# One decoder layer in fp32 on one core: the second MLP product's weights are loaded from POOL's queue

## The chip, the core and the metric

The kernel runs on one core of a Trainium2 chip. The metric is the device time of one execution in microseconds (us). TensorE (PE) multiplies, VectorE (DVE), ScalarE (ACT) and GpSimd (POOL) work on tiles, and SyncE (SP) does nothing but issue transfers (DMAs). POOL and ACT can issue DMAs as well. All DMAs of the core run on the same 16 DMA engines. The profile shows the DMAs that SP issues in queue q1 (hardware_dynamic) and those that POOL issues in queue q0 (software_dynamic).

## The reference

One layer, sequence 1024, width 1024, everything float32:

```python
h = x @ w_in                                  # columns: pool | q | k | v | forget gate
mix = concat(pool_mixer(h), forgetting_attention(h)) @ w_out
x = layer_norm(ALPHA * x + mix, ln1_g, ln1_b)
hid = square(relu(x @ w_mlp1))                # 1024 x 4096
x = layer_norm(ALPHA * x + hid @ w_mlp2, ln2_g, ln2_b)
```

The last line holds the second MLP product, `hid @ w_mlp2`: 1024 tokens by 4096 by 1024. Its weights are 16 MB, called `w2` in the kernel (`in_w_dram` in the profile, where the numbers in names are left out, so that `w1` and `w2` share that name).

## The kernel before

Every fp32 operand of a product is split into a high and a low part (`split`, L70: ACT makes the high part at L71, DVE the low one at L72), and each product is done as three matmuls. Both MLP products use a two-by-two block scheme with seven products in place of eight: the blocks of weights and activations are first added and subtracted into the versions B11, B21, T1 to T4 and B22 and A11 to A22, S1 to S4.

**First MLP product (`Unit`, L735, PE's line L727).** Sixteen units of 256 hidden columns. Each unit makes seven products, squares the result, forms the sums and splits them. POOL stores the split activations to `hid_dram` (L852 and L865, seven stores of 512 KB a unit). One unit, the kept one, stays in SBUF.

**Second MLP product (`Pair` and `Step`, L958 and L1020, PE's line L1060).** A `Pair` is the two 128-row blocks of `w2` that belong to a unit: `load_f` and `load_g` fetch 512 KB each into buffers of tag `S`, of which there are three (`NBUF`, L48). `split_b`, `sums`, `split_t2`, `split_t13` and `split_t4b` turn them into the seven weight versions. A `Step` is one group of two token tiles with up to four pairs, plus the kept unit in the first four steps. `Step.load` (L1028) brings the split activations back from `hid_dram` into buffers of tags `Q` and `A`, 256 KB a load, 128 KB for the group A22. `load_x` (L1047) brings a row tile of the first norm's output into an `S` buffer, to be added as the residual. Each step makes seven products (`p1` to `p7`), adds them to the rows `y`, and the last four steps norm and store them; there POOL multiplies and adds the norm's rows (`on_pool`, L601).

The steps of a pair are hung on places in the chain of units and steps: `load_f` and `load_g` on the step before the one that first uses the pair. For the pair that a step starts with, the code reads:

```python
at(i - 1, 4 * k, p.load_f)
at(i - 1, 2 + 3 * k, p.load_g)
at(i - 1, 3 + 3 * k, p.split_b)
```

Two things set the order. Each engine carries out its own instructions in the order in which a scheduler laid them down, and a DMA issue is an instruction of the engine that issues it: it waits in that engine's queue for its buffer to be free, and all that stands behind it in the queue waits with it. A load into an `S` buffer waits for the last split that reads the buffer's former contents.

Of the kernel before, what the change touches and what calls it, by code (L numbers as in the profile page):

```python
# [36 lines left out]
def trunk(ctx, tc, xT, xn, wuqk, wvf, bf, poolw, pscale, wout, g1, b1, w1, w2, g2, b2, out):  # L37
# [5 lines left out]
    nc = tc.nc  # L43
# [7 lines left out]
    def slot(tag, shape, dt=F32R):  # L51
        uid[0] += 1
        return sb.tile([P] + list(shape), dt, tag=tag, bufs=NBUF[tag], name=f"{tag}{uid[0]}")
# [9 lines left out]
    def bank(tag=None):  # L63
        uid[0] += 1
        if tag is None:
            tag = CYCLE[rr[0] % 8]
            rr[0] += 1
        return ps.tile([P, CH], F32, tag=tag, bufs=PBUF[tag], name=f"{tag}{uid[0]}")
# [134 lines left out]
    for t in range(4, NT):  # L203
        for half in range(2):
            b = bank()[:, 0:VW]
# [432 lines left out]
    for n, unit in enumerate(order):  # L638
        p = n // 8
# [95 lines left out]
    class Unit:  # L735
# [6 lines left out]
        def load_f(self):  # L742
            self.f = slot("S", [2, H, P], F32)
            nc.sync.dma_start(self.f.rearrange("p b k f -> p (b k) f"), w1[2 * self.u])

        def load_g(self, tag="S"):
            self.g = slot(tag, [2, H, P], F32)
            nc.sync.dma_start(self.g.rearrange("p b k f -> p (b k) f"), w1[2 * self.u + 1])
# [209 lines left out]
    class Pair:  # L958
# [4 lines left out]

        def load_f(self):
            self.f = slot("S", [2, CH], F32)
            nc.sync.dma_start(self.f.rearrange("p b n -> p (b n)"), w2[2 * self.u])

        def load_g(self, tag="S"):
            self.g = slot(tag, [2, CH], F32)
            nc.sync.dma_start(self.g.rearrange("p b n -> p (b n)"), w2[2 * self.u + 1])  # L970

        def put(self, name, hi, lo, raw):
            self.v[name] = (hi, lo)
# [285 lines left out]
```

## Time and profile before

| | us |
|---|---|
| median of 3 runs (1038.8 to 1041.12) | 1039.55 |
| profiled execution | 1042.56 |
| its span, first to last instruction | 1040.8 |
| PE busy in the span | 1019.3 |
| DVE busy | 757.1 |
| ACT busy | 514.1 |
| POOL busy | 154.7 |

The prediction's rows come from these views. A *timeline* row is: start in us, length in us, engine, line, operation, output<-inputs, shape, count, and in brackets the idle time of the engine before it with what ended it. "SPq" is SP's queue: its rows are issues. A *waits* row is: engine, line and tile that waited, what it waited for, us in total, number of times, longest. The *chain of waits* follows the work that ended last back in time: start, length, what. A *windows* row is a stretch, its length, then for PE, PEld (weight loads of PE), DVE, ACT and POOL the busy us with the number of instructions, then the granted clock of PE, the busy share of the 16 DMA engines and GB/s. A *groups* row has, after the bar, busy us and mean ns, and then the idle time before with its causes. A *DMA* row of a queue has packets, MB and share of the engines; one of an issue has count, KB each and median us from issue to landing.

### The profile page before, as it was taken

What the parts mean: (1) busy time and instruction counts of PE and PEld (TensorE: products, weight loads), DVE (VectorE), ACT (ScalarE), POOL (GpSimd) and SP (SyncE); (2) the same over time, 40 slices, a digit from 0 to 9 for tenths busy, and PEclk for the clock granted to TensorE, in tenths of its full rate; (3) what the DMA queues carried; (4) which work ended last, traced back from release to release, by engine and by line L of the source; (5) the groups of instructions that cost most, each with busy time, mean ns of one, the idle gap of its engine ahead of it and who ended that gap; (6) DMA issues with size and microseconds to landing.
All of it is one profiled execution on the core that took longest, in us unless ns stands there. A gap on an engine that the chain in (4) does not pass through costs nothing.

```text
span 1040.8 us, 14125 instructions
## 1 busy us (share of the span) xinstructions
PE 1019.3 (98%) x4976; PEld 847.3 (81%) x4976; DVE 757.1 (73%) x1300; ACT 514.1 (49%) x823; POOL 154.7 (15%) x267
## 2 busy tenths in 40 slices
PE   9999999999999999999999999999999999999996
PEld 9988888888768888887888888888788888888884
DVE  4776678677767887989778778888775666565547
ACT  4623666666664332676766766668521221122152
POOL 0200112111100031112122121120100000000047
PEclk9999999999999999999999999999999999999998
DMA  9702311112585523239667667665989888878753
GB/s 352 279 28 85 113 59 36 40 40 58 176 273 150 183 113 102 75 131 362 241 260 265 224 261 262 223 252 197 350 285 307 285 259 286 275 224 272 238 187 121
DMA packets 113670, 206.29 MB, mean 198 GB/s; under 512 B 9592, under 2 KB 78008, under 8 KB 113600
## 3 DMA queue, kind: packets, MB, share of 16 engines
q1 hardware_dynamic: 94608, 137.63, 41.1%
q0 software_dynamic: 18560, 67.12, 16.6%
q8 instruction: 39, 0.64, 0.3%
q10 hardware_dynamic: 432, 0.66, 0.2%
q14 instruction: 31, 0.25, 0.1%
HBM read 132.42 MB, written 72.94 MB: 197 GB/s over the span
## 4 chain that ended last, share of the span: by engine, by line
PE 50%; issue 4%; DVE 3%; DMA 1%; POOL 1%; SPq 0%; ACT 0%; DVEq 0%; POOLq 0%
PE s L1060 15%; PE pv L1060 8%; PE s L727 8%; PE mm L727 6%; PE pt L727 6%; PE pv L727 4%; PE pt L1060 2%; PE mm L1060 2%; DMA hid_dram<-A 1%; DMA A<-hid_dram 1%; DVE B L72 1%; POOL hid_dram L852 0%; POOL A L720 0%; SPq L1039 0%; DVE A L850 0%
## 5 line engine op out<-in xcount | busy, mean ns | idle before, releaser
L71 ACT CAST B<-S 128x1024 fp32r<-128x1024 f32 (+1 forms) x78 | 67.8, 881 | 163.2 <-PE s L1060 62.8
L727 PE MATMUL s<-B,Q 128*128 128x512 f32 x492 | 116.4, 389 | 0.2 <-ACT B L71 0.2
L727 PEld LDWEIGHTS s<-B,Q 128*128 128x128 f32 x492 | 92.3, 188 | 19.7 <-ACT B L71 0.7
L72 DVE TENSOR_TENSOR B<-S,B 128x1024 fp32r<-128x1024 f32 (+1 forms) x78 | 78.0, 1008 | 31.0 <-ACT B L71 30.8
L1060 PE MATMUL s<-B,Q 128*128 128x512 f32 x390 | 94.7, 389 | 0.0
L1060 PE MATMUL s<-B,A 128*128 128x512 f32 x333 | 84.0, 397 | 2.3 <-DMA A<-hid_dram 2.3
L1060 PEld LDWEIGHTS s<-B,Q 128*128 128x128 f32 x390 | 73.2, 188 | 15.5
L71 ACT CAST Q<-S 128x1024 fp32r<-128x1024 f32 x53 | 55.7, 1051 | 57.3 <-PE s L727 17.0
L852 POOL DMA_DIRECT2D hid_dram<-A x90 | 48.1, 537 | 221.4 <-ACT A L849 164.5
L1060 PEld LDWEIGHTS s<-B,A 128*128 128x128 f32 x333 | 63.1, 190 | 17.1 <-DMA A<-hid_dram 2.7
L72 DVE TENSOR_TENSOR Q<-S,Q 128x1024 fp32r<-128x1024 f32 x53 | 65.6, 1238 | 15.2 <-ACT Q L71 14.7
L727 PE MATMUL pt<-B,Q 128*128 128x512 f32 x312 | 74.6, 389 | 0.0
L727 PE MATMUL mm<-B,Q 128*128 128x512 f32 x300 | 71.6, 389 | 0.0
L727 PEld LDWEIGHTS pt<-B,Q 128*128 128x128 f32 x312 | 58.5, 188 | 12.1
L727 PEld LDWEIGHTS mm<-B,Q 128*128 128x128 f32 x300 | 56.3, 188 | 11.7
L377 ACT ACTIVATE A<-A,nm 128x1024 f32<-128x1024 f32 (+7 forms) x64 | 49.7, 777 | 32.3 <-DVE nm L375 31.0
L416 PE MATMUL pv<-A,B 128*128 128x256 f32 x320 | 62.2, 295 | 2.8 <-DVE A L399 1.2
L416 PEld LDWEIGHTS pv<-A,B 128*128 128x128 f32 x320 | 51.0, 188 | 17.1 <-ACT A L398 7.0
L399 DVE TENSOR_TENSOR A<-pt,A 128x512 fp32r<-128x512 f32 (+1 forms) x80 | 49.6, 634 | 15.1 <-ACT A L398 14.5
L850 DVE TENSOR_TENSOR A<-A,A 128x1024 f32<-128x1024 f32 x45 | 53.6, 1220 | 0.0
L362 POOL TENSOR_TENSOR A<-A,maskb 128x128 f32<-128x128 f32 x48 | 23.4, 491 | 190.8 <-DVE nm L375 135.2
L398 ACT CAST A<-pt 128x512 fp32r<-128x512 f32 (+1 forms) x80 | 41.5, 543 | 19.2 <-PE pt L397 18.3
(427 smaller groups left out, 2342.0 us busy)
## 6 DMA issues: line engine op xcount, KB each, us to landing
hid_dram<-A POOLq DMA_DIRECT2D x105, 512.0 KB, 4.0
S<-in_w_dram SPq DMA_DIRECT2D x62, 512.0 KB
Q<-hid_dram SPq DMA_DIRECT2D x101, 256.0 KB
A<-hid_dram SPq DMA_DIRECT2D x79, 256.0 KB
S<-in_wuqk_dram SPq DMA_DIRECT2D x12, 512.0 KB
wo_dram<-Q POOLq DMA_DIRECT2D x10, 512.0 KB, 3.8
B<-wo_dram SPq DMA_DIRECT2D x10, 512.0 KB
A<-ncf_dram SPq DMA_DIRECT2D x8, 512.0 KB
```

The lines of the kernel that those rows point to most:

```text
L71: nc.scalar.copy(hi, src)
L72: nc.vector.tensor_tensor(lo, src, hi.bitcast(F32), ALU.subtract)
L362: nc.gpsimd.tensor_tensor(nb[:, qs], nb[:, qs], maskb, ALU.add)
L377: nc.scalar.activation(pt[:, :nk], pt[:, :nk], AF.Exp, bias=nm, scale=-1.0, accum_out=rsum[h][:, i : i + 1])
L398: nc.scalar.copy(tt[:, 0, ev], tp[:, ev])
L399: nc.vector.tensor_tensor(tt[:, 1, ev], tp[:, ev], tt[:, 0, ev].bitcast(F32), ALU.subtract)
L416: nc.tensor.matmul(ov, V[j][:, h].rearrange("p s d -> p (s d)"), tt[:, s, a:b], start=(j == 0 and s == 0), stop=(j == 2 * m + 1 and s == 1),)
L727: nc.tensor.matmul(dst, b[x][:, k], A[a][y][:, k], start=first and k == 0 and i == 0, stop=k == H - 1 and i == 2, skip_group_check=not first,)
L850: nc.vector.tensor_tensor(x, x, hi.bitcast(F32), ALU.subtract)
L852: nc.gpsimd.dma_start(hid_dram[self.u, :, i, AT[name] : AT[name] + 2 * CH], part.rearrange("p q n t -> p (q n t)"))
L1060: nc.tensor.matmul(dst, h[:, p_], w[q_], start=first and u == self.us[0] and j == 0, stop=u == self.us[-1] and j == 2, skip_group_check=no ...
```

## The change

`Pair.load_f` and `Pair.load_g` issue their DMA from POOL's queue instead of SP's. Nothing else in the source is touched: sizes, buffers and what is computed stay.

```diff
         def load_f(self):
             self.f = slot("S", [2, CH], F32)
-            nc.sync.dma_start(self.f.rearrange("p b n -> p (b n)"), w2[2 * self.u])
+            nc.gpsimd.dma_start(self.f.rearrange("p b n -> p (b n)"), w2[2 * self.u])
 
         def load_g(self, tag="S"):
             self.g = slot(tag, [2, CH], F32)
-            nc.sync.dma_start(self.g.rearrange("p b n -> p (b n)"), w2[2 * self.u + 1])
+            nc.gpsimd.dma_start(self.g.rearrange("p b n -> p (b n)"), w2[2 * self.u + 1])
```

There are 32 such loads, one for each 128-row block of `w2`. The first of them that stand behind the last stores of the first product, on POOL (numbers in names are those of the buffers, `w2` stands under its own name here):

```order
 L852 DMA hid_dram_3781<-A1239_6906 128x1024
 L852 DMA hid_dram_3781<-A1232_6870 128x1024
+L966 DMA S1265_7030<-in_w2_dram 128x1024
+L970 DMA S1269_7056<-in_w2_dram 128x1024
+L966 DMA S1281_7133<-in_w2_dram 128x1024
+L970 DMA S1285_7163<-in_w2_dram 128x1024
```

After the last two stores POOL's queue now holds 26 weight loads in a row, up to the norms of the last steps. The six loads before these stand in pairs and fours between the stores of the last units.

The same place in SP's queue, where the first steps' activations are loaded:

```order
 L1039 DMA Q1262_7016<-hid_dram_3781 128x2x256 x2
-L966 DMA S1265_7030<-in_w2_dram 128x1024
 L1039 DMA Q1277_7115<-hid_dram_3781 128x2x256
 L1039 DMA A1264_7027<-hid_dram_3781 128x2x256 x2
 L1039 DMA A1268_7053<-hid_dram_3781 128x2x128 x2
-L1039 DMA A1272_7073<-hid_dram_3781 128x2x256
-L970 DMA S1269_7056<-in_w2_dram 128x1024
-L1039 DMA A1272_7073<-hid_dram_3781 128x2x256
+L1039 DMA A1272_7073<-hid_dram_3781 128x2x256 x2
 L1039 DMA A1273_7076<-hid_dram_3781 128x2x256
```

Two weight loads leave; the second stood between the two loads into the buffer A1272. The order of the activation loads themselves is the same here.

The scheduler also lays down a few of VectorE's instructions in another order, the first of them here (L1070 adds a product to the rows `y`, L72 splits, L985 begins a pair's sums):

```order
 L72 TENSOR_TENSOR B1267_7050<-S1249_6952,B1267_7050 128x1024
+L1070 TENSOR_TENSOR A1244_6931<-A1244_6931,pv1263_7019 128x512
 L72 TENSOR_TENSOR B1271_7068<-S1265_7030,B1271_7068 128x512
-L1070 TENSOR_TENSOR A1244_6931<-A1244_6931,pv1263_7019 128x512
+L72 TENSOR_TENSOR B1275_7109<-S1253_6971,B1275_7109 128x1024
 L985 TENSOR_TENSOR S1265_7030<-S1265_7030 128x512
-L72 TENSOR_TENSOR B1275_7109<-S1253_6971,B1275_7109 128x1024
 L986 TENSOR_TENSOR U1274_7085<-S1269_7056,S1265_7030 128x512
```

An addition and a split move ahead of work on the newly loaded buffer S1265. The split of S1253 (B1275_7109) is the last reader of the buffer into which the next weight load, S1281_7133, goes. PE's order is the same before and after.

## The prediction

> **What bounds the kernel now.** I read the engines' totals first, then the windows by stage, then PE's waits, and last the queues around the one wait that was left.
>
> ```profile
> PE 1019.3 (98%) x4976; PEld 847.3 (81%) x4976; DVE 757.1 (73%) x1300; ACT 514.1 (49%) x823; POOL 154.7 (15%) x267
> PE s L1060 <- DMA A<-hid_dram: 2.3, 1, 2.3
> ```
>
> The second row is all that PE waits for between 477 and 1027 us, in the two MLP products. The changed loads serve the second one, L1060, from 711 us on. So the change can win or lose there only by that one hole of 2.30 us, by what follows from it, or by opening new ones.
>
> ```profile
> 746.55 0.85 PE L1060 MATMUL s<-B,A 128*128 128x512 f32 x3
> 749.71 2.01 PE L1060 MATMUL s<-B,A 128*128 128x512 f32 x6 [2.30 <-DMA A<-hid_dram]
> 742.89 6.78 DMA A<-hid_dram
> 749.71 5.44 PE s L1060 x15
> 801.80 5.45 PE s L1060 x24
> 746.00:751.00 5.00, 2.70 (x12) 1.72 (x11) 1.98 (x4) 1.87 (x3) 0.00 (x0) 1.00 1.06 357
> 751.00:754.50 3.50, 3.50 (x10) 2.69 (x9) 2.85 (x4) 0.40 (x1) 0.00 (x0) 0.51 0.96 306
> ```
>
> The first two rows are PE's timeline, the next three the chain of waits, the last two windows (PE, PEld, DVE, ACT, POOL busy, granted clock, DMA share, GB/s). PE waits for an activation load that SyncE issued at 742.89 and that took 6.78 us to land. After the hole the granted clock is 0.51 for 3.5 us: 15 matmuls take 5.44 us, where 24 take 5.45 at the full clock (0.227 each, 3.41 for 15). So the hole costs 2.30 + (5.44 - 3.41) = **4.33 us** in this execution. A shorter hole costs no clock:
>
> ```profile
> 30.73 0.39 PE L83 MATMUL s<-A,B 128*128 128x260 f32 x1 [1.49 <-ACT B L71]
> 31.00:37.00 6.00, 6.00 (x51) 6.00 (x51) 6.00 (x15) 6.00 (x10) 1.03 (x2) 1.00 0.41 162
> ```
>
> 1.49 us of waiting left the clock at 1.00. The step is somewhere between 1.49 and 2.30 us.
>
> This execution took 1042.56 us (span 1040.8 and 1.76 around it), the runs have a median of 1039.55, 3.0 us less. Taking the whole hole off the profiled time gives 1038.2, and the runs shown lie at 1038.8 to 1041.12. If nothing else differs between a profiled and a plain execution, a plain one holds some 0.6 to 2.9 us of the hole, 1.3 at the median. That is an estimate from two figures; I use it as the likelier reading, not as known.
>
> **Why that load is late.** SyncE's queue in order of time, and the windows:
>
> ```profile
> 733.58 0.34 SPq L966 DMA_DIRECT2D S<-in_w_dram  x1
> 737.22 0.53 SPq L1039 DMA_DIRECT2D Q<-hid_dram  x1
> 737.98 4.21 SPq L1039 DMA_DIRECT2D A<-hid_dram  x5
> 742.30 0.54 SPq L970 DMA_DIRECT2D S<-in_w_dram  x1
> 742.89 2.52 SPq L1039 DMA_DIRECT2D A<-hid_dram  x4
> 748.99 0.33 SPq L966 DMA_DIRECT2D S<-in_w_dram  x1
> 735.00:741.00 6.00, 6.00 (x28) 4.99 (x27) 5.95 (x9) 3.49 (x5) 0.00 (x0) 1.00 1.02 395
> 741.00:746.00 5.00, 5.00 (x24) 4.14 (x23) 3.44 (x5) 2.78 (x4) 0.00 (x0) 1.00 1.04 343
> 746.00:750.00 4.00, 1.70 (x8) 1.11 (x7) 0.98 (x2) 0.87 (x2) 0.00 (x0) 1.00 1.05 357
> ```
>
> A weight load of 512 KB stands directly ahead of the late one (742.30), which is what the change takes out of that queue. But the last figures matter more: from 735 to 750 us the 16 DMA engines are full (share 1.02 to 1.05, 343 to 395 GB/s). What lands when is set there by bytes, not by who issues.
>
> **The change part by part.**
>
> *SyncE loses 32 issues* of 0.33 to 0.54 us (rows above). SyncE does nothing but issue, so this frees time but is on the path only where SyncE is late. At the hole it is worth 742.89 - 742.30 = 0.59 us of earlier issue. With the DMA engines full I count 0 of it.
>
> *POOL gains 32 issues.* The price is that of its stores:
>
> ```profile
> L852 POOL DMA_DIRECT2D hid_dram<-A x41 | 21.9, 540 | 98.7 <-ACT A L849 65.9 <-DVE A L850 19.1 <-issue 13.3
> 730.93 1.69 POOL L852 DMA_DIRECT2D hid_dram<-A  x3
> 996.22 2.40 POOL L612 TENSOR_TENSOR Q<-Q,S 128x1024 f32<-128x1024 f32 x1 [263.60 <-ACT Q L611]
> ```
>
> 32 x 0.54 = 17 us, of which 26 issues fall into the 263.6 us in which POOL has nothing to do: 0. The other six stand between stores. Would a load that waits for its buffer hold a store up there? The second and the sixth of them in SyncE's queue of before, and the store that comes next:
>
> ```profile
> 690.82 0.33 SPq L970 DMA_DIRECT2D S<-in_w_dram  x1
> 692.36 0.53 POOL L852 DMA_DIRECT2D hid_dram<-A  x1 [10.06 <-ACT A L849]
> 719.04 1.02 SPq L970 DMA_DIRECT2D S<-in_w_dram  x1
> 726.90 0.53 POOL L852 DMA_DIRECT2D hid_dram<-A  x1 [24.42 <-ACT A L849]
> ```
>
> The stores go out 1.5 us (690.82 to 692.36) and 7.9 us (719.04 to 726.90) later, so the loads are gone by then. Cost 0. If the 1.5 us were gone, a store would slide by as much, into the 24.42 us in which POOL waits before 726.90: still 0.
>
> *The weights come another way.* Do they arrive in time? At a middle step:
>
> ```profile
> 787.33 0.33 SPq L966 DMA_DIRECT2D S<-in_w_dram  x1
> 788.47 0.33 SPq L970 DMA_DIRECT2D S<-in_w_dram  x1
> 793.01 0.62 ACT L71 CAST B<-S 128x512 fp32r<-128x512 f32 x1 [0.65 <-DMA S<-in_w_dram]
> 801.63 2.90 PE L1060 MATMUL s<-B,A 128*128 128x512 f32 x12
> hid_dram<-A POOLq DMA_DIRECT2D x86, 512.0 KB, 3.8
> 476.00:711.00 235.00, 234.12 (x1033) 193.91 (x1034) 192.04 (x242) 161.26 (x202) 47.51 (x86) 1.00 0.69 257
> ```
>
> The second load lands at 793.0, its split's first half ends at 793.6, and the step that first uses this pair begins at 801.6: 8.0 us of cover. Loads of this size from POOL's queue are not in the trace; its stores of 512 KB landed in 3.8 us (median of 86) with VectorE busy for 192 of 235 us, against 4.5 us for 788.47 to 793.0. Bounds: -0.7 us each by that, +8.0 before PE sees anything. Cost 0.
>
> The Trainium skill (SBUF — State Buffer, section "SBUF: two separate sides") speaks against the change: POOL writes the descriptors of its own DMAs, and is locked out while VectorE runs an operation in a two-port mode; it gives 620 ns alone and 3100 ns beside a copy. By it a load would come 2.5 us later (an estimate from that page), which the 8.0 us swallow; the stores' 3.8 us do not show the lock.
>
> *The bytes at the hole.* The weight loads of 733.58 and 742.30 are wanted by then either way, so the bytes ahead of the late load don't shrink. They can grow: the next weight load (748.99 in SyncE's queue) needs only its buffer, which VectorE frees here:
>
> ```profile
> 744.15 1.22 DVE L72 TENSOR_TENSOR B<-S,B 128x1024 fp32r<-128x1024 f32 x1
> ```
>
> at 745.4. POOL can issue it then, 3.6 us earlier, beside the late load and the one after it. 524 KB at 357 GB/s are 1.47 us. Bounds for the hole: from -4.33 us (it closes) to +1.47 and, if that carries a short hole over the step, another 2.03 of half clock. How two queues share the engines is seen where stores met activation loads (each queue's packets, MB and share of the engines in stretches of 0.5, 1 and 1 us):
>
> ```profile
> q1 hardware_dynamic: 130, 0.12, 69.2%
> q0 software_dynamic: 22, 0.09, 43.7%
> q0 software_dynamic: 96, 0.39, 99.5%
> q1 hardware_dynamic: 263, 0.26, 72.7%
> q0 software_dynamic: 49, 0.14, 34.6%
> ```
>
> From 732.0 both, from 732.5 POOL's nearly alone, from 733.5 SyncE's ahead again: they take turns, 0.26 MB of activations against up to 0.5 MB of the other. In its own queue the weight load of 742.30 goes earlier, its successor takes a turn too, and the late load moves little: I count from 740 us, after the last stores. There are 1.5 MB of activations (the loads issued from 737.22 up to the late one: five of 256 KB, two of 128), 1.05 MB of weights and up to 0.52 of the successor. At the 0.37 MB/us between the windows' 343 and 395, 2.55 MB take 6.9 us and 3.07 MB 8.3: from 746.9 to 748.3. PE asks at 747.2 (746.55 and three matmuls of 0.227), so 0 to 1.1 us of hole. The plain runs seem to hold 0.6 to 2.9 already, 1.3 at the median. Against that I take 1.0 for the hole, between the middle of my count and its end, since the engines don't finish all at once: **-0.3 us**.
>
> The Trainium skill (DMA: Bandwidth & Descriptors, section "Queues, rings and completion order") states that an engine goes round the queues that have work, a packet of several descriptors each; the three stretches agree. By it the activations lose up to two thirds of an engine while weights are in flight, which is the slower rival below.
>
> **Sum:** 0 + 0 + 0 + 0 - 0.3 on 1039.55: **1039.2 us**.
>
> **Rivals.** *The hole closes.* With no weights in its queue the late load lands before 747.2. For it: the 512 KB directly ahead of it, and a latency of 6.78 us. Against: the full DMA engines. It takes up to 4.33 us, if the runs hold as much as the profile: 1035.2; if they hold 1.3, 1038.2. As a case of its own it stands for the first kind, 1035.2 to 1037.4, in the middle 1036.3. Chance 0.20.
>
> *Weights push ahead of activations*, slower: the successor's 1.47 us go in front of the load PE waits for. From the point where the hole passes 1.49 to 2.30 us, the clock halves too: 1039.55 + 1.47 + 2.03 = 1043.1. For it: runs with a hole of about 1.3 would cross. Against: activations have 0.59 us of earlier issue and the queue to themselves. Chance 0.17.
>
> *Loads from POOL are slow through the whole stage*: past 8.0 us each further us is lost at each of some 13 steps, so 1 us more is 1052. Nothing in the stores speaks for it: 0.03.
>
> *SyncE's queue was never what anything waited for*, so that moving the loads does nothing: that is the forecast itself, with the rest 0.60.
>
> **The numbers.** Two executions of this kernel differ by up to 2.3 us here, so about 0.2% (2.1 us) is what can be told from no change. Faster 0.20, same 0.60, slower 0.20. The forecast's own range is 1037.6 to 1041.5. The range for 8 in 10 leaves out the far half of each rival: 1036.3 to 1042.4.
>
> **What would show it.** q0's 67.12 MB grow by 32 x 0.524 to 83.9 and SyncE's queue keeps only L1039 and L1051. POOL's L966 appears near 745 instead of SyncE's at 749. Right: one PE wait on hid_dram near 747 us, from nothing to 2.5 us, and no other in L1060; ACT and DVE still wait for S loads, PE never for them. Hole closed and time under 1037.4: the first rival. Hole over 2.3 us, or a second one between 747 and 760 us: the second. PE waiting on ACT or DVE at every step: the third. A PE wait outside 720 to 770 us would be something I have not seen.

## The result and the profile after

| | before | after |
|---|---|---|
| median of the timed runs (6 each) | 1040.34 us | 1046.97 us |
| their spread | 1038.8 to 1043.64 | 1045.78 to 1048.68 |
| profiled execution | 1042.56 | 1048.68 |
| its span | 1040.8 | 1046.9 |

The change makes the kernel slower: ratio 1.0059, 95% interval 1.0040 to 1.0079. The forecast was 1039.2 with a range up to 1042.4. It was wrong in sign and size.

The page of the changed kernel, its engines, its two queues, and the loads by what issues them (the last figure is the median us from issue to landing):

```profile
PE 1019.9 (97%) x4976; PEld 846.2 (81%) x4976; DVE 756.3 (72%) x1300; ACT 514.0 (49%) x823; POOL 171.7 (16%) x299
q1 hardware_dynamic: 90000, 120.85, 36.1%
q0 software_dynamic: 23168, 83.90, 21.3%
S<-in_w_dram POOLq DMA_DIRECT2D x31, 512.0 KB, 5.2
```

The change was made as described: q0 has 83.9 MB, POOL 17 us more of issues. The engines do the same work as before. So the 6 us are waits, and the waits of TensorE after 480 us say which (engine, line, tile, what it waited for, us in total, times, longest):

```profile
PE pv L1060 <- DVE Q L1070: 2.1, 1, 2.1
PE pv L1060 <- DVE A L1070: 1.5, 1, 1.5
PE s L1060 <- DMA A<-hid_dram: 1.0, 1, 1.0
```

The old wait on `hid_dram` is still there, shorter. Two new ones, longer than it, are on VectorE: on additions of a product to the rows `y` (L1070), which free the only `pv` bank. TensorE's timeline has them at 763.02 and 781.79, and the windows show the clock behind the second:

```profile
749.35 1.78 PE L1060 MATMUL s<-B,A 128*128 128x512 f32 x6 [1.03 <-DMA A<-hid_dram]
763.02 1.67 PE L1060 MATMUL pv<-B,A 128*128 128x512 f32 x6 [1.53 <-DVE A L1070]
781.79 4.51 PE L1060 MATMUL pv<-B,A 128*128 128x512 f32 x12 [2.06 <-DVE Q L1070]
783.00:786.40 3.40, 3.40 (x9) 2.62 (x9) 1.20 (x3) 0.00 (x0) 0.00 (x0) 0.50 1.06 339
```

**Why VectorE's addition is late.** Here are VectorE's rows at the first of them, of the changed kernel and then of the kernel before:

```profile
760.47 0.69 DVE L986 TENSOR_TENSOR U<-S,S 128x512 f32<-128x512 f32 x1 [3.66 <-DMA S<-in_w_dram]
761.08 0.69 DVE L72 TENSOR_TENSOR B<-S,B 128x512 fp32r<-128x512 f32 x1
761.68 0.69 DVE L988 TENSOR_TENSOR S<-S,S 128x512 f32<-128x512 f32 x1
762.28 0.68 DVE L1070 TENSOR_TENSOR A<-A,pv 128x512 f32<-128x512 f32 x1
```

```profile
760.27 0.68 DVE L1070 TENSOR_TENSOR A<-A,pv 128x512 f32<-128x512 f32 x1
760.87 0.69 DVE L72 TENSOR_TENSOR B<-S,B 128x512 fp32r<-128x512 f32 x1
761.48 0.69 DVE L986 TENSOR_TENSOR U<-S,S 128x512 f32<-128x512 f32 x1
```

In the changed kernel the addition stands *behind* L986, which needs a weight load. VectorE waits 3.66 us for that load with the addition queued behind it, and TensorE waits for the addition. In the kernel before, the addition comes first. This is the scheduler's doing, in the piece of VectorE's order that the part on the change did not show:

```
 L1070 TENSOR_TENSOR A1259_6998<-A1259_6998,s1266_7032 128x512
 ...
+L986 TENSOR_TENSOR U1287_7189<-S1285_7163,S1281_7133 128x512
+L72 TENSOR_TENSOR B1286_7174<-S1285_7163,B1286_7174 128x512
+L988 TENSOR_TENSOR S1281_7133<-S1285_7163,S1281_7133 128x512
 L1070 TENSOR_TENSOR A1258_6997<-A1258_6997,pv1278_7117 128x512
-L72 TENSOR_TENSOR B1286_7174<-S1285_7163,B1286_7174 128x512
-L986 TENSOR_TENSOR U1287_7189<-S1285_7163,S1281_7133 128x512
-L988 TENSOR_TENSOR S1281_7133<-S1285_7163,S1281_7133 128x512
```

The dots stand for three instructions (L72, L985, L72, at 757.81 to 759.14 us) that stood here before and now stand ahead of the first line. What moved ahead reads newly loaded weights. That the scheduler counts on an earlier landing from the freed queue is my reading; the runs show the order, not its reason.

The second wait has one more link. VectorE and POOL of the changed kernel, then VectorE and SyncE's queue of the kernel before:

```profile
772.10 0.69 DVE L72 TENSOR_TENSOR B<-S,B 128x512 fp32r<-128x512 f32 x1 [5.60 <-ACT B L71]
772.71 0.68 DVE L1070 TENSOR_TENSOR Q<-Q,s 128x512 f32<-128x512 f32 x1
773.91 1.22 DVE L1054 SCALAR_TENSOR_TENSOR Q<-S,Q 128x1024 f32<-128x1024 f32 x1
775.43 0.54 POOL L970 DMA_DIRECT2D S<-in_w_dram  x1 [8.69 <-DMA Q<-hid_dram]
779.24 0.69 DVE L986 TENSOR_TENSOR U<-S,S 128x512 f32<-128x512 f32 x1 [2.37 <-DMA S<-in_w_dram]
781.05 0.68 DVE L1070 TENSOR_TENSOR Q<-Q,pv 128x512 f32<-128x512 f32 x1
```

```profile
768.26 0.69 DVE L1070 TENSOR_TENSOR Q<-Q,s 128x512 f32<-128x512 f32 x1 [1.96 <-PE s L1060]
768.98 1.22 DVE L1054 SCALAR_TENSOR_TENSOR Q<-S,Q 128x1024 f32<-128x1024 f32 x1
770.23 0.33 SPq L970 DMA_DIRECT2D S<-in_w_dram  x1
```

A split of newly loaded weights (L72) now stands ahead of the addition of the residual row (L1054). L1054 ends at 775.1 where it ended at 770.2. It is the last reader of an `S` buffer, so the next weight load goes out at 775.43 where it went out at 770.23, and L986 and the next `pv` addition come 4.6 us later. (The row puts POOL's wait down to a `Q` load. But the issue comes 0.30 us after L1054's end, as in order_kept below, where it comes from 766.23 to 766.53 and the row names L1054.)

**The end of the program.** TensorE's last matmul ends 3.8 us later than before, the span 6.1 us. The other 2.3 us are behind the last work, in the launch's closing line (L1255; duration in ns min/median/max, first and last start), before and after:

```profile
L1255 POOLq DRAIN  x3: 45/93/4658, 1035.0 to 1040.5; - x3
L1255 SPq DRAIN  x3: 7/7/7, 1040.0 to 1040.3; - x3
```

```profile
1038.86 1.26 POOL L625 TENSOR_TENSOR A<-A,S 128x512 f32<-128x512 f32 x1
L1255 POOLq DRAIN  x3: 45/102/7270, 1038.8 to 1046.6; - x3
L1255 SPq DRAIN  x3: 7/7/40, 1044.1 to 1046.3; - x3
L1255 POOLq EVENT_SEMAPHORE  x4: 17/17/17, 1046.1 to 1046.8; - x4
```

POOL's drain begins with its last operation and takes 7.27 us, to 1046.1. SyncE's first drain is at 1044.1. The closing semaphores come behind POOL's drain, POOL's own at 1046.1. In the kernel before, POOL's drain is over at 1039.7, 0.3 us ahead of SyncE's. I call what is left of it after POOL's last operation the drain. That operation is the addition of L625, about 1.30 us (the expectations call it the last multiply). This gives 3.4 us before and 6.0 us after.

The two profiles add up: +0.9 us that the first 480 us took longer (why was not looked into), -2.9 at the old wait (its length, and a clock that stayed at 1.00), +1.7 and +2.4 at the new ones, +1.7 of half clock, +2.3 at the end: 6.1 us.

### The profile page after: what moved, and what is told of

It reads as the page before. It is cut to its first block, busy times and chain, and to the rows that moved or that the text cites. A ratio compares the mean times of both kernels' runs of the same rounds, so it can differ in the third digit from the quotient of the medians.

```text
span 1046.9 us, 14139 instructions
## 1 busy us (share of the span) xinstructions
PE 1019.9 (97%) x4976; PEld 846.2 (81%) x4976; DVE 756.3 (72%) x1300; ACT 514.0 (49%) x823; POOL 171.7 (16%) x299
## 4 chain that ended last, share of the span: by engine, by line
PE 47%; issue 6%; DVE 3%; DMA 2%; POOL 1%; DVEq 0%; ACT 0%; POOLq 0%
PE s L1060 14%; PE s L727 8%; PE pv L1060 7%; PE mm L727 6%; PE pt L727 6%; PE pv L727 4%; PE mm L1060 2%; PE pt L1060 2%; DMA S<-in_w_dram 1%; DMA hid_dram<-A 1%; DVE B L72 1%; POOL hid_dram L852 1%; POOL A L720 0%; DVE bns L573 0%; DVE A L850 0%
## 5 line engine op out<-in xcount | busy, mean ns | idle before, releaser
L72 DVE TENSOR_TENSOR B<-S,B 128x1024 fp32r<-128x1024 f32 (+1 forms) x78 | 78.1, 1007 | 37.4 <-ACT B L71 37.1
L72 DVE TENSOR_TENSOR Q<-S,Q 128x1024 fp32r<-128x1024 f32 x53 | 65.6, 1237 | 14.6 <-ACT Q L71 14.0
```

Of the source, the lines that this page charges most:

```text
L72: nc.vector.tensor_tensor(lo, src, hi.bitcast(F32), ALU.subtract)
```

## The experiments

**VectorE's order put back** (order_kept). Edges of issue order tie each of a few instructions to the one that stood ahead of it before:

```diff
-        trunk(tc, *args, out)
+        trunk(tc, *args, out); in_order(tc, nc.cur_bb.bb.instructions)
...
+def in_order(tc, instructions):
+    traced = {i.name: i for i in instructions}
...
+    for row in ORDERS:
+        for first, then in zip(row, row[1:]):
+            tc.add_manual_dep(traced[then], first, info, reason="order")
```

> The change as it is, but with edges of issue order that put VectorE's and ScalarE's instructions back into the order of the kernel before (VectorE in three stretches of 31, 9 and 7 instructions, ScalarE in one of 5); TensorE's order is the same in both anyway. Theory O (order): the two new TensorE waits on VectorE (1.54 us at 763.02, 2.06 us at 781.79 and about 1.7 us of half clock after it, 5.3 us together) come from adds that stand behind operations on weights not yet landed. They go; the one on hid_dram near 749 stays near 1.0 us; POOL's drain at the end stays long (about 6 us after its last multiply, 2.3 us past the rest). Time 1046.97 - 5.3 = about 1041.7. Theory Q (queue): weights from POOL's queue land too late or push ahead of the activations, whatever VectorE's order. Then TensorE still waits 3 us or more between 755 and 790 and the time stays at 1045.5 to 1047.5.

Measured: 1042.16 us, ratio 1.0020 (1.0010 to 1.0029). TensorE's waits after 477 us and the end:

```profile
PE s L1060 <- DMA A<-hid_dram: 1.1, 1, 1.1
L1255 POOLq DRAIN  x3: 45/93/7270, 1031.1 to 1038.8; - x3
```

Both new waits are gone with the loads still on POOL's queue. This is 4.8 us of the loss by the medians (4.1 by the two ratios), and the weights' way does not cost it by itself. The long drain stays.

**The order alone** (sp_reordered). The loads stay on SyncE's queue, and the same kind of edges lay down the changed kernel's order.

> The kernel before, all weight loads on SyncE's queue, but with VectorE's and ScalarE's instructions in the order of the changed kernel (TensorE's order kept; some of SyncE's later activation loads, those of tiles numbered 1318 to 1347, stand in a slightly other order). Theory O: the order alone opens TensorE waits on VectorE near 763 and 782 us, 3.6 us and up to 2 us of half clock, beside the old wait of up to 2.3 us on hid_dram; POOL's drain at the end stays at about 3.4 us after its last multiply and hides. Time 1044 to 1046. Theory Q: nothing but the queue matters, and this one is unchanged: 1040.3, no wait on VectorE.

Measured: 1043.57 us, ratio 1.0037 (1.0025 to 1.0050).

```profile
PE pv L1060 <- ACT A L1068: 1.8, 1, 1.8
757.08 0.97 PE L1060 MATMUL pv<-B,B 128*128 128x512 f32 x3 [1.84 <-ACT A L1068]
758.50:762.00 3.50, 3.50 (x11) 2.68 (x10) 3.50 (x7) 1.67 (x2) 0.00 (x0) 0.51 0.99 311
```

The order alone costs 3.4 us without any change of queue, but not by the two waits of the changed kernel: neither is there. Its new wait comes one place earlier than expected, beside 1.6 us on `hid_dram`: ScalarE's copy of a `pv` bank (L1068) had also been moved behind casts of newly loaded weights. The size was 0.4 us under the range.

So the two waits need the queue as well. The load behind the first of them and ScalarE's cast that waits for it, in the changed kernel and then in this one:

```profile
753.40 0.54 POOL L970 DMA_DIRECT2D S<-in_w_dram  x1 [6.89 <-DVE B L72]
760.40 0.62 ACT L71 CAST B<-S 128x512 fp32r<-128x512 f32 x1 [5.20 <-DMA S<-in_w_dram]
```

```profile
752.72 0.33 SPq L970 DMA_DIRECT2D S<-in_w_dram  x1
757.38 0.62 ACT L71 CAST B<-S 128x512 fp32r<-128x512 f32 x1 [0.35 <-DMA S<-in_w_dram]
```

From POOL's queue this load took 7.0 us, from SyncE's 4.7. The load of the split ahead of L1054, at the second wait, took 5.2 us (766.20 to 771.45) against 3.4 (764.74 to 768.14). With the old order the same two loads from POOL's queue took 6.3 and 5.7 us (order_kept), and TensorE waited for neither. So each of the two waits takes both, weights that land later and an addition queued behind them. A reading of why they land later, which no run tests: SyncE's queue, rid of the weight loads, runs ahead. It sent the residual row (L1051) at 755.64 where it was 760.39 before, and moved 0.97 and 0.96 MB in the two halves of those 7.0 us, beside 0.52 MB of weights.

**What makes the drain long** (tiny1, tiny128). 32 DMAs without use, two beside each `load_g`, on POOL's queue of the kernel before, first of one row, then of 128 rows:

```diff
+            [nc.gpsimd.dma_start(sb.tile([1, 4], F32, tag="tiny", bufs=2, name=f"tiny{uid[0]}_{k}"), w2[2 * self.u + 1][:1, :4]) for k in range(2)]
```

> The kernel before with 32 more DMAs on POOL's queue, each of 16 bytes from one row of w2 into a scratch tile that nothing reads, two beside each load_g; orders of TensorE, VectorE and ScalarE are as before. Theory D1 (drain by issues): the last drain of POOL grows with the number of DMAs that POOL has issued, by 2.6 us for 32: 6.0 us after POOL's last multiply where before has 3.4, the end of the program waits for it, and the time is 1040.3 + 2.3 = 1042.6. Theory D2 (drain by bytes or descriptors, or by something else in the changed kernel): 3.4 us, time 1040.3.

> As the run with 16-byte DMAs, but each of the 32 is 128 rows of 32 bytes, so as many rows as a weight load has, with almost no bytes. D1 (by issues): the same 6.0 us and 1042.6 as with one row. By rows: 6.0 us here and 3.4 us with one row. By bytes: 3.4 us in both, 1040.3. The work on TensorE, VectorE and ScalarE should not change in any of these cases.

Measured: 1044.46 (1.0044) and 1047.29 (1.0075). Both times are spoiled: the scheduler put the DMAs at the program's start, where POOL's late work made TensorE wait, 2.3 us with one row.

```profile
PE s L244 <- DVE Q L235: 2.3, 1, 2.3
L1255 POOLq DRAIN  x3: 51/103/5220, 1035.2 to 1041.0; - x3
L1255 POOLq DRAIN  x3: 51/93/6940, 1037.8 to 1045.2; - x3
```

But the drains (one row, then 128) are told apart: 0.6 us more with one row, 2.3 with 128. So neither issues alone nor bytes, but mostly rows. All 32 went out in the first 70 us, so the drain does not wait for anything still under way; it pays for DMAs issued 970 us earlier.

**How the drain grows** (half_kept, fewer_pinned, one_pair; all with VectorE's and ScalarE's order put back). Half the loads on POOL; then all loads there, but 16 stores of the first norm moved away from it; then one pair alone:

```diff
+            (nc.gpsimd if self.u % 2 else nc.sync).dma_start(self.f.rearrange("p b n -> p (b n)"), w2[2 * self.u])
...
-        nm.on_vector(nc.gpsimd)
+        nm.on_vector(nc.sync)
...
+            (nc.gpsimd if self.u == ORDER[3] else nc.sync).dma_start(self.f.rearrange("p b n -> p (b n)"), w2[2 * self.u])
```

> Only the loads of the odd pairs, 16 of the 32, go to POOL's queue; VectorE and ScalarE in the order of the kernel before, as in order_kept. TensorE should wait only on hid_dram near 749 us, 1.0 to 1.6 us. What is tested is POOL's drain at the end. If each weight load adds its 2.6/32 = 0.08 us, it lasts 3.4 + 1.3 = 4.7 us after POOL's last multiply, 1.0 us past the rest: 1040.2 - 0.4 + 1.0 = 1040.8. If the drain jumps at some count between 136 and 168 issues: 3.4 us (1039.8) or 6.0 us (1042.1).

> order_kept, and the 16 stores of the first norm's rows (128 rows of 2 KB each) go out from SyncE's queue instead of POOL's, so that POOL issues 152 DMAs, 32 of them weight loads; VectorE and ScalarE keep the order of before at that place too. If stores that POOL has issued lengthen its last drain as loads do, it lasts 6.0 - 1.3 = 4.7 us and the time is 1042.2 - 1.3 = 1040.9. If only the loads count, 6.0 us and 1042.2. The stores are 400 us away from the second product; TensorE should not see them.

> Only the two loads of the fourth pair (the ones issued at 733.58 and 742.30 us in the kernel before, of which the second stands ahead of the activation load that TensorE waits for at 749.71) go to POOL's queue; VectorE and ScalarE in the order of before. POOL's drain grows by 2 x 0.08 us and stays hidden. If taking those 512 KB out of SyncE's queue helps the late activation load, the hole is under 1.0 us and the time 1039.0 to 1039.9; if bytes alone set the landing, the hole is 1.0 to 1.6 us as in all other runs and the time 1040.2 within 0.5.

```profile
L1255 POOLq DRAIN  x3: 45/93/5965, 1034.9 to 1041.4; - x3
L1255 POOLq DRAIN  x3: 45/102/6045, 1035.6 to 1042.2; - x3
L1255 POOLq DRAIN  x3: 45/93/4817, 1032.4 to 1037.7; - x3
```

The drains came as the straight line said: a weight load adds 0.08 us (2.6/32, 1.3/16, 0.16/2), a store of 128 rows of 2 KB takes away 0.077. The times were 1042.51 (1.0019), 1043.95 (1.0035) and 1040.11 (1.0007, 0.9997 to 1.0016). The first two missed by 1.7 and 3.0 us. In the profile of the first the wait on `hid_dram` was 1.9 us with a halved clock. In the second SyncE's queue had come out in another order too, and TensorE waited 0.2 to 1.0 us at four new places; which made which was not tried. One pair on POOL's queue changes nothing that can be measured; its profile has a wait of 1.3 us on `hid_dram` and one of 0.5 us on a `pv` addition. The pair was not the one that the expectation names: POOL issued its two loads at 744.97 and 751.99, which are those of 748.99 and 753.28 in the kernel before, and the load ahead of the late one stayed in SyncE's queue, at 741.47. So this run does not test what that load does there.

**The late activation load** (swap_sp, and the same kernel again as swap_again; before_prof). In the kernel before, edges put the weight load of 742.30 us four places back in SyncE's queue.

> The kernel before, with the weight load of 742.30 us moved behind the next four activation loads in SyncE's own queue (a few later loads of that queue move by one place too); orders of VectorE and ScalarE are kept, and one matmul on TensorE moves past nine others. If the 512 KB ahead of it make the late activation load late, it lands up to 524 KB / 0.37 MB per us = 1.4 us earlier, TensorE's hole near 749 is at most 0.5 us, and the time is 1039.0 to 1039.9. The weights land about as much later; if that matters, TensorE waits on VectorE near 757 to 763 us and the time is above 1041.

Measured: 1039.55 (0.9997, 0.9989 to 1.0006) and, the second time, 1039.80 (0.9989, 0.9980 to 0.9998). The wait on `hid_dram` is gone from both profiles, and new ones on the weights are 0.2 to 0.8 us. So the 512 KB ahead of it did make that load late, and it helps to let them go later; to let them go from another queue at the same time left waits of 1.0 and 1.1 us (the changed kernel, order_kept). Yet the median gains only 0.4 us each time. How long the wait is in the kernel before:

> The kernel before, for a second profile (the first repeat fell into an execution in which every matmul took twice its time). Hole near 749 us of 1.0 to 1.6 us with the clock at 1.0 after it, PE's last matmul ends near 1028, if the first profile was a draw at the long end; a hole of 2.3 us and 1031, if that is its usual length.

Measured: 1041.00 (1.0001), hole 1.64 us at a full clock, TensorE's last matmul at 1028.2. (An earlier repeat took 2060 us and can't be compared.) In seven further profiles with that queue's head unchanged the wait was 0.6 to 2.2 us, 1.5 at the median. The first profile was a draw at the long end.

**ScalarE's queue instead** (act_kept).

```diff
+            nc.scalar.dma_start(self.f.rearrange("p b n -> p (b n)"), w2[2 * self.u])
```

> All 32 weight loads from ScalarE's queue, with most of VectorE's order of before (24 of its instructions and 36 of TensorE's stand otherwise). POOL's drain stays at 3.4 us. If the weights only need a queue apart from the activations, and no software drain, the time is 1039.0 to 1040.0. If a load that waits for its buffer holds up ScalarE's casts and copies behind it, TensorE waits on ACT in the second product and the time is 1041 to 1046.

Measured: 1049.82 us, ratio 1.0086 (1.0073 to 1.0099), above the range. Waits after 700 us:

```profile
PE pv L1060 <- DVE Q L1070: 3.9, 3, 3.3
PE s L1060 <- DMA A<-hid_dram: 2.6, 1, 2.6
PE pv L1060 <- DVE A L1070: 0.6, 1, 0.6
```

The drain stays at 3.4 us here, but the order is not the old one: the edges of order_kept are in this kernel, yet 24 of VectorE's instructions and 36 of TensorE's stand otherwise, and the `pv` additions are late again. I did not put these back, so what the queue itself would cost is open. The Trainium skill (DMA: Bandwidth & Descriptors, section "SWDGE vs HWDGE vs iDMA") sends plain transfers to SyncE or ScalarE. For SyncE against POOL these runs agree; ScalarE was the slowest place of the three.

**What the drain costs in the time** (tiny_mid, swap_tiny; best, swap_tiny2). 32 useless DMAs of 128 rows, now pinned behind stores of the first product, first in the kernel before, then in the one with the weight load moved back:

```diff
+    def tiny(i, name, u): i and (name != "A12" or u < 2) and tc.keep_in_program_order(nc.gpsimd.dma_start(sb.tile([128, 8], F32, tag="tiny", bufs=2, name=f"tiny{name}{u}"), w2[u][:, :8]))
...
             for i, part in enumerate((hi.bitcast(F32), x)):
...
+                tiny(i, name, self.u)
```

> The kernel before with 32 more POOL DMAs of 128 rows of 32 bytes each, into a scratch tile that nothing reads, each pinned behind a store of the first product, between 450 and 730 us, where POOL waits for several us between stores. TensorE's and ScalarE's orders are as before, two of VectorE's instructions change places. If POOL's drain at the end costs time, it lasts 5.6 us after POOL's last multiply (as with the same DMAs at the program's start), ends 2.0 us past the rest, and the time is 1040.0 + 2.0 = 1042.0 with TensorE's waits unchanged. If the drain is only a row of the profile that nothing waits for, 1040.0.

> swap_sp with the 32 tiny POOL DMAs of tiny_mid; two of VectorE's instructions change places, all else is ordered as in swap_sp. If the drain is paid in full, it ends 2.0 us past the rest and the time is 2.0 us over swap_again's: 1041.6. If it costs nothing or the DMAs speed something up, within 0.5 us of swap_again.

Measured: 1040.70 (1.0002, 0.9993 to 1.0011), and 1040.04 (0.9996, 0.9988 to 1.0005) where its base took 1039.80 on the same chip. Both drains ended 2.1 us past the rest in the profile, so 2 us were expected and 0.2 to 0.7 came. Part of the answer is at the first product's start: a wait that takes 1.1 to 1.3 us in the kernels before and in the changed one is 0.2 to 0.3 us in these two, in which two of VectorE's instructions had changed places. The last two runs separate this:

> swap_sp with two of VectorE's instructions in the first product exchanged (a subtraction of L850 ahead of a split of L72), as the scheduler had put them in swap_tiny, and no added DMAs: it differs from swap_tiny by the 32 tiny DMAs alone. The wait near 476 us shrinks from 1.2 to 0.3 us: 1039.7 - 0.9 = 1038.8, faster than the kernel before by 0.13%. If the drain is paid, it is 2.1 us under swap_tiny's 1040.04, near 1038.0; if the drain costs nothing, equal to swap_tiny.

> swap_sp with the 32 tiny POOL DMAs and VectorE's order kept everywhere, so that nothing but the DMAs is added. If the drain is paid in full: 1039.7 + 2.1 = 1041.8, and 3.0 us over best. If it costs nothing: 1039.7, and 0.9 us over best.

Measured: 1039.50 (0.9990, 0.9981 to 0.9998) and 1041.43 (1.0013, 1.0003 to 1.0022). Their drains, in that order:

```profile
L1255 POOLq DRAIN  x3: 45/93/4660, 1031.0 to 1036.5; - x3
L1255 POOLq DRAIN  x3: 45/102/7103, 1030.6 to 1038.3; - x3
```

With the order kept everywhere, the DMAs cost 1.6 to 1.9 us against the three runs without them (1039.50, 1039.55, 1039.80; the first with the two instructions exchanged): the drain is paid, at nearly its 2.1 us. The first of the two missed: the exchange alone left the wait at 1.1 us, so what shortened it in the other two is open. All three runs without added DMAs are a little faster than the kernel before, by 0.03 to 0.11%, at the edge of what can be told.

**Fewer issues than before** (before_fewer, stores_sp: one kernel, first a single profile, then timed). The 16 stores of the first norm on SyncE's queue of the kernel before:

> The kernel before with the 16 stores of the first norm's rows issued by SyncE: POOL issues 120 DMAs, 16 fewer. The time is not the point (VectorE's order changes in that stage). 136, 138, 152 and 168 issues gave drains of 3.36, 3.52, 4.66 to 4.75 and 5.97 us, 0.08 per issue. If the straight line goes on, 3.36 - 1.3 = 2.1 us after POOL's last multiply; if 3.4 us is a floor, 3.4.

> The kernel before with the 16 stores of the first norm's rows on SyncE's queue (VectorE's and ScalarE's order differ in that stage), timed. Its drain of 2.1 us gains nothing, since that of before is already hidden by 0.3 us. If nothing else changes, 1040.0; its single look took 1038.57, within the spread of the kernel before.

```profile
L1255 POOLq DRAIN  x3: 45/102/3433, 1031.0 to 1036.5; - x3
```

The line goes on below the kernel before: 3.43 - 1.30 = 2.1 us. Timed, it took 1039.33 (0.9988, 0.9979 to 0.9998), 0.7 us less than expected and 0.9 less than the kernel before beside it; the drain cannot be why, since it was hidden already. I have no cause for that gain.

## Why the prediction was wrong

*What bounds the kernel, and how much of the hole a plain run holds*: held. The estimate of 1.3 us stands beside the median of 1.5 in the seven profiles. Taking the wait away gained less, 0.4 us, with small new waits in its place.

*SyncE loses 32 issues, 0*: held for the issues' own time at the hole. What the sum has no term for is that SyncE's queue, no longer held up, sends later transfers earlier (the residual row by 4.7 us), beside the weights. *The bytes at the hole*: held. 1.0 us was taken for its length, and 1.03 and 1.1 us came with all weights on POOL's queue. "What lands when is set there by bytes, not by who issues" agrees with both edits of that load: another queue left the wait, a later issue closed it.

*The weights come another way, "Cost 0"*: the step that failed most, 4.8 us by putting the order back. (The order alone costs 3.4 us, at another place.) Its bound of -0.7 us for a load's landing had the wrong sign where it counted: the two loads at the new waits took 2.3 and 1.8 us longer than with the same order on SyncE's queue. The 8.0 us of cover were measured from the load to the TensorE step that *uses* the weights. The weights' first consumers are VectorE and ScalarE, which work in order: whatever stands behind such an operation waits for the load too, and among that were additions that free the `pv` bank. The cover that counted ran from the landing to VectorE's turn. It was below zero at 760.47, where VectorE waited 3.66 us. That costs nothing by itself (in the kernel before VectorE waits 3.65 us at 749.02): it costs when an addition that TensorE needs stands behind it, as it does in the new order and did not in the old. The rows of the new order were at hand. The part on the change showed only the first piece of it, and the prediction priced none.

*POOL gains 32 issues, 0*: failed by 2.3 us in the profile, 1.6 to 1.9 us as 32 other DMAs price it. I asked where the issues' own time lies, and it is hidden as said. I did not look at the end of the program, where the rows of the kernel before already show POOL's drain ending 0.3 us ahead of the last other engine.

*The clock step between 1.49 and 2.30 us*: does not hold as a matter of the wait's length alone. Waits of 1.53 and 1.64 us left the clock at 1.00; 1.84, 1.87 and 2.06 us halved it for about 3.4 us:

```profile
750.50:754.00 3.50, 3.50 (x17) 2.89 (x16) 2.25 (x3) 0.12 (x1) 0.00 (x0) 1.00 1.07 331
751.00:754.50 3.50, 3.50 (x10) 2.75 (x9) 2.72 (x4) 0.27 (x1) 0.54 (x1) 0.53 1.10 341
```

These are the windows behind 1.64 us (the kernel before, second profile) and 1.87 us (half the loads on POOL). But in act_kept a wait of 2.56 us left the clock at 1.00 (9 matmuls in 2.52 us), and one of 3.27 us halved it (12 in 5.49):

```profile
749.51 2.52 PE L1060 MATMUL s<-B,A 128*128 128x512 f32 x9 [2.56 <-DMA A<-hid_dram]
879.37 5.49 PE L1060 MATMUL pv<-B,A 128*128 128x512 f32 x12 [3.27 <-DVE Q L1070]
```

What decides beside the length is open. The Trainium skill (TensorE: Matmul & The Clock Gate, "Part 1: The HAM clock gate") lets the clock fall after at least one idle window of about 3.4 us. The slow stretches have that length, but waits of little over half of it brought them on; the rows decide.

*The rivals*: none was right. The slower one, weights ahead of activations, expected a longer wait on `hid_dram` and got a shorter one; in the rows above it is the weights that land late beside activations. "A PE wait outside 720 to 770 us would be something I have not seen" is what came, at 781.79.

## What to carry to other kernels

A DMA that is moved to another queue also moves instructions on engines that the diff does not name, where a scheduler sets their order: read every piece of the new order, and ask of each operation that waits for a transfer what is queued behind it and who waits for that. Ask too what the queue that it leaves will send earlier. Measure a load's cover to its first consumer's turn, not to the engine that needs the final product. And look at the program's last microseconds: work that is free in the middle can still be paid for at the end.

## What the hardware showed that was not expected

- POOL's drain at the end grows with the DMAs that POOL issued, however long ago: 2.1, 3.4, 3.5, 4.7 and 6.0 us after its last operation for 120, 136, 138, 152 and 168 issues. An issue of 128 rows costs 0.071 to 0.076 us with rows of 32 bytes, 0.077 with 2 KB and 0.082 with 4 KB; one of a single row 0.018. The line does not pass through zero (it would meet it near 95 issues), and what the drain does is not known from these runs.
